# Attention heads' operands prepared one softmax earlier, and two stores moved in a queue, in a DeepNorm decoder layer

## The chip, the cores and the metric

One NeuronCore of a Trainium2 chip. The metric is the device time of one execution in microseconds, the median of three runs.

## The reference

One layer over x of 512 tokens by 1024 channels, all in float32:

- `proj = x @ w_in`, split into q, k, v (512 columns each), the pooling input (512) and two gates (1024 each).
- Branch A: causal attention, 8 heads of 64 channels, with a relative position bias. With 512 tokens and blocks of 256 the block selection keeps every earlier key, so it is plain causal softmax attention over 4 tiles of 128 queries.
- Branch B: trailing means over 2, 4, 8 and 16 tokens in four groups of 128 channels, minus the token, times a small matrix per group.
- Each branch is projected to 1024 channels (`w_branch_attn`, `w_branch_pool`), weighted by the sigmoid of its gate, and the two are added; the sum goes through `w_out`.
- `h = LayerNorm(alpha * x + ...)`; then a gated MLP of width 2816 with a causal convolution of width 3 on the gate path, and `LayerNorm(alpha * h + f)`.

## The kernel before

Every large product is made from float32 operands cut into a high and a low part (`split`: ACT copies the high part, DVE subtracts, lines 77 and 78), and is three matmuls per tile (`mm3`, lines 253, 256 and 257). Weights come in chunks of 128 x 1024 (512 KB). A chunk's raw tile is loaded by the SP queue into one of three buffers (`wraw`), split into one of five slots (`whi`, `wlo`), and used; `weights(i)` fetches up to three chunks ahead.

The order in which each engine works is settled when the kernel is built. A planner keeps a simulated clock and lets each engine take, among the instructions that it holds to be ready, the one that stands first in the program. `tc.issue_after(ins)` adds an edge to that plan: what the block issues on the engine of `ins` stands behind `ins` in that engine's queue. On the chip the engines then run their queues in this order and wait on semaphores. Queues of DMA issues (SP, ACT, POOL) are in the same plan.

**The attention stage.** For each of the 8 heads:

- `head(h)` (lines 441 to 457) makes the operands of the scores in four half-height operations: K1, the high part of k (ACT, L451), KL, the low part (DVE, L452), Q1, the high part of the scaled q (ACT, L453), with its low part in the other 64 partitions (DVE, L454). Two DMAs issued by SP (L457) copy the halves of K1 and KL into the other partitions. Q1, K1 and KL have three buffers each.
- `scores(h)` is eight matmuls, with K1 (L550) and with KL (L551), four DVE reductions that add the bias strip and take the row minimum of the negated scores (L554, the last of them is `nms[h]`), four exponentials on ACT (L559, the last is `exps[h]`), a reciprocal (L561) and four scalings on POOL (L564).
- `trans(h)` transposes the probabilities on PE (L634) and copies them out (L636 to L638); `pv(p)` multiplies a pair of heads with the values (L647, tile `ob`).
- `cover(h)` is a product of another branch put between the heads, so that PE has work during a softmax: a gate tile for the first two, then the pooling branch's projection, 12 matmuls into a bank `br` and a copy by ACT (`br_done`, L622).

The loop of line 669 runs, for h from 0 to 7: `cover(h)`, `scores(h + 2)`, `head(h + 3, nms[h + 2], exps[h + 1])`, the pair's `pv`, `trans(h)`. The last two arguments of `head` are the instructions behind which its work is put: on DVE behind the reductions of head h + 2, on ACT behind the exponentials of head h + 1.

**The last product.** The second MLP matrix is applied in seven products of 11 slices (`product`, line 1058; T3, B11, B21, T1, T2, B22, T4), each with six weight chunks. Some products load their chunks through SP into `wraw` (L236 in `fetch_fo`); others use a resident tile `tw` to which the next block of weights is added by DMAs from POOL (L241). During the sixth product the second norm's rows (scale and bias, broadcast to all partitions, tile `lnb`) are loaded by POOL (L782). Two stores issued by SP (L1107) write the bias row into rows 0 to 255 of the result, and `scale_out` later adds the normed rows to it with an accumulating DMA from POOL (L834). The last two row tiles are finished and stored without that.

Of the kernel before, what the change touches and what calls it, by code (L numbers as in the profile page):

```python
# [14 lines left out]
P = 128  # L15
# [4 lines left out]
H = 8  # L20
# [33 lines left out]
def layer_kernel(ctx: ExitStack, tc: tile.TileContext, xT, x, w_v, w_c, rel_bias, invcnt, w_group,  # L54
                 pscale, w_br, w_out, lnr, w_fi, convp, w_fo, out):
    nc = tc.nc
# [12 lines left out]
    def flip(v):  # L69
        (pst, pn), (_, n) = v.ap  # L70
        return bass.AP(tensor=v.tensor, offset=v.offset + P - 1, ap=[[pst, pn], [P, n // P], [-1, P]])

    def split(hi, lo, src, copy=None):
        if copy:
            copy(hi, src)
        else:
            state["hi"] = nc.scalar.activation(hi, src, AF.Copy)  # L77
        state["lo"] = nc.vector.tensor_tensor(lo, src, hi.bitcast(F32), op=ALU.subtract)  # L78
        return state["lo"]
# [53 lines left out]
    def slot(i, n, near=False):  # L133
        o = BESIDE if near else 0
        return tuple(wp.tile([P, SLOT], F32R, tag=f"w{q}", name=f"w{q}{i}", bufs=RING)[:, o:o + n]
                     for q in ("hi", "lo"))

    state = {"next": 0, "limit": WO0 - 1}
# [83 lines left out]
    def half(name, sl):  # L222
        return w_fo[int(name[1]) - 1, 2 - int(name[2])][:, sl]

    def piece(c):
        return slice(c * D, min((c + 1) * D, KH * S))

    def fetch_fo(i, name, c):
        sl = piece(c)
        n = sl.stop - sl.start  # L230
        step = {"T3": "=B11", "B11": "+B12", "T1": "+B22", "T2": "+B21", "T4": None}
        if name in step:
            raw = tw[:, sl]
        else:
            raw = wp.tile([P, D], F32, tag="wraw", name=f"wraw{i}", bufs=3)[:, :n]
            nc.sync.dma_start(raw, half(name, sl))  # L236
        hi, lo = slot(i, n)
        split(hi, lo, raw)
        then = step.get(name)
        if then and then[0] == "+":  # L240
            nc.gpsimd.dma_start(raw, half(then[1:], sl), accum_op=ALU.add)  # L241
        elif then:
            nc.sync.dma_start(raw, half(then[1:], sl))
        return hi, lo
# [196 lines left out]
    def head(h, *behind):  # L441
        p, e = divmod(h, 2)
        own, oth = slice(e * DH, (e + 1) * DH), slice((1 - e) * DH, (2 - e) * DH)
        qb, kb = raw_q[p], raw_k[p]
        Q1[h] = av.tile([P, S], F32R, tag="q1", name=f"q1_{h}")
        K1[h] = av.tile([P, S], F32R, tag="k1", name=f"k1_{h}")
        KL[h] = av.tile([P, S], F32R, tag="kl", name=f"kl_{h}")
        with ExitStack() as held:
            for ins in behind:
                held.enter_context(tc.issue_after(ins.ins))  # L450
            nc.scalar.activation(K1[h][own, :], kb[own, :], AF.Copy)  # L451
            nc.vector.tensor_tensor(KL[h][own, :], kb[own, :], K1[h][own, :].bitcast(F32), op=ALU.subtract)  # L452
            nc.scalar.activation(flip(Q1[h][own, :]), qb[own, :], AF.Copy, scale=DH ** -0.5)  # L453
            nc.vector.scalar_tensor_tensor(flip(Q1[h][oth, :]), qb[own, :], DH ** -0.5,  # L454
                                           flip(Q1[h][own, :]).bitcast(F32), op0=ALU.mult, op1=ALU.subtract)
        for t in (K1[h], KL[h]):
            nc.sync.dma_start(t[oth, :].bitcast(F32), t[own, :].bitcast(F32))  # L457
# [36 lines left out]
    def in_tile(kind, j):  # L494
        wh, wl = split3(weights(at[kind, j]), KT)
        b = bank(f"{kind}{j}")
        for kt in range(KT):
            mm3(b, (wh[:, kt, :], wl[:, kt, :]), (xT_hi[:, kt, :], xT_lo[:, kt, :]), kt == 0, kt == KT - 1)
        return b
# [34 lines left out]
    nms = {}  # L534
    exps = {}
# [3 lines left out]
    def scores(h):  # L539
        if h + 2 < H:  # L540
            load_strip(h + 2)
        pp = aw.tile([P, 10 * P], F32, tag="pp", name=f"pp{h}")
        nm = aw.tile([P, NT], F32, tag="nm", name=f"nm{h}")
        rs = aw.tile([P, NT], F32, tag="rs", name=f"rs{h}")
        b01 = bank(f"sc{h}_01")
        dst = [b01[:, :2 * P], b01[:, 2 * P:], bank(f"sc{h}_2")[:, :3 * P], bank(f"sc{h}_3")]
        for i in range(NT):
            n = max(2, i + 1) * P
            q = slice(i * P, (i + 1) * P)
            nc.tensor.matmul(dst[i], Q1[h][:, q], K1[h][:, :n], start=True, stop=False)  # L550
            nc.tensor.matmul(dst[i], Q1[h][:, q], KL[h][:, :n], start=False, stop=True)  # L551
        for i in range(NT):
            n = (i + 1) * P
            nms[h] = nc.vector.tensor_tensor_reduce(out=pp[:, offs[i]:offs[i] + n], in0=dst[i][:, :n],  # L554
                                                    in1=strips[h][:, S - n:], scale=1.0, scalar=3.0e38,
                                                    op0=ALU.add, op1=ALU.min, accum_out=nm[:, i:i + 1])
        for i in range(NT):
            n = (i + 1) * P
            exps[h] = nc.scalar.activation(pp[:, offs[i]:offs[i] + n], pp[:, offs[i]:offs[i] + n], AF.Exp,  # L559
                                           scale=-1.0, bias=nm[:, i:i + 1], accum_out=rs[:, i:i + 1])  # L560
        nc.vector.reciprocal(rs, rs)  # L561
        for i in range(NT):
            n = (i + 1) * P
            nc.gpsimd.tensor_scalar(pp[:, offs[i]:offs[i] + n], pp[:, offs[i]:offs[i] + n], rs[:, i:i + 1], 1.0,  # L564
                                    op0=ALU.mult, op1=ALU.mult)
        Ps[h] = pp
# [44 lines left out]
    def br_mm(f, br, b=None, ks=range(4), pin=False):  # L611
        i, o = at["br", (f, br)]
        wh, wl = (t[:, o:o + S].rearrange("p (a c) -> p a c", a=4) for t in weights(i))
        b = b or bank(f"br{f}_{br}")
        for k in ks:
            src = (zT_hi[:, k, :], zT_lo[:, k, :]) if br else (oT_hi[:, k, :], oT_lo[:, k, :])
            mm3(b, (wh[:, k, :], wl[:, k, :]), src, k == 0, k == 3, pin and k == ks[0])
        return b

    def br_done(f, br, b):  # L620
        t = branch[f, br] = unused.pop(0)
        nc.scalar.activation(t, b, AF.Copy)  # L622
# [18 lines left out]
    def pv(p):  # L641
        b = bank(f"ob{p}")
        for kb in range(NT):
            n = (NT - kb) * P
            for e in range(2):
                h = 2 * p + e
                state["pv"] = nc.tensor.matmul(b[e * DH:(e + 1) * DH, kb * P:], vv[:, kb, h * DH:(h + 1) * DH],  # L647
                                 PTs[h][:, toff[kb]:toff[kb] + n], start=kb == 0, stop=kb == NT - 1)
        split(oT_hi[:, p, :], oT_lo[:, p, :], b)
# [6 lines left out]
    def cover(h):  # L656
        with ExitStack() as held:
            if h < H - 1:
                for ins in (nms[h + 1], exps[h + 1]):
                    held.enter_context(tc.issue_after(ins.ins))  # L660
            if h < 2:
                state["limit"] = at["g", KT] + h
                nc.vector.tensor_copy(plain_gate[:, h, :], in_tile("g", h * KT))
            else:
                f = h - 2
                state["limit"] = at["br", (min(f + 3, KT - 2), 1)][0]
                br_done(f, 1, br_mm(f, 1))

    for h in range(H):
        cover(h)  # L670
        if h + 2 < H:
            scores(h + 2)
        if h + 3 < H:
            head(h + 3, nms[h + 2], exps[h + 1])
        with ExitStack() as held:
            if h and h % 2 == 0:
                pv(h // 2 - 1)
                held.enter_context(tc.issue_after(state["pv"].ins))
            trans(h)
        if h == 0:  # L680
            with tc.issue_after(nms[2].ins), tc.issue_after(exps[1].ins):
                for k in range(4):
                    split(zT_hi[:, k, :], zT_lo[:, k, :], zT[:, k, :])
# [96 lines left out]
    def ln_rows(r):  # L780
        t = hw.tile([P, 2, D], F32, tag="lnb", name=f"lnb{r}")
        nc.gpsimd.dma_start(t, bass.AP(tensor=lnr.tensor, offset=lnr.offset + r * D, ap=[[0, P], [D, 2], [1, D]]))  # L782
        nc.gpsimd.tensor_scalar(t[:, 0, :], t[:, 0, :], -0.5, None, op0=ALU.mult)
        return t

    lnb = ln_rows(0)
# [316 lines left out]
    gather(3, S, D, bank_a[1], 1, False, False)  # L1103
    product(5, bank_d, False)
    lnb = ln_rows(2)
    for i in range(2):
        nc.sync.dma_start(out[i * P:(i + 1) * P, :], lnb[:, 1, :])  # L1107
    gather_all(bank_d, (0, 0, -1, False, True))
    for i in range(2):
        scale_out(i)  # L1110
# [89 lines left out]
```

## Time and profile before

| | us |
|---|---|
| median of 3 runs | 630.85 (630.69 to 631.05) |
| the profiled execution | 631.2 |
| its span, first to last instruction | 629.5 |
| PE busy | 615.7 (98%) |
| DVE busy | 510.1 (81%) |
| ACT busy | 360.1 (57%) |
| POOL busy | 104.2 (17%) |

PE is TensorE's matmuls and PEld its weight loads; DVE, ACT, POOL and SP are the vector, scalar, GpSimd and sync engines. In rows of the timeline the columns are the start, the duration, the engine, the line, the operation, output <- inputs with shapes, and the number of instructions merged in the row; square brackets give the idle time in front of it and what ended that. A `q` behind an engine's name (SPq) is its queue of DMA issues.

### The profile page before, as it was taken

How to read it: one execution, taken by the hardware profiler on the slowest of the kernel's cores; microseconds unless marked ns; L12 is line 12 of the kernel's file. 1: busy time of each engine (PE TensorE's matmuls, PEld its weight loads, DVE VectorE, ACT ScalarE, POOL GpSimd, SP SyncE). 2: the span in 40 equal slices, each digit the busy share in tenths (PEclk: the TensorE clock that was granted, in tenths of full speed). 3: DMA queues.
4: the chain of work that ended last, by engine and by line, in shares of the span. 5: the costliest groups of instructions: out<-in, count | busy, mean ns of one | idle time of the engine just before them, and what ended most of it. 6: DMA issues, size and time to landing. Idle time of an engine off the chain costs nothing.

```text
span 629.5 us, 10658 instructions
## 1 busy us (share of the span) xinstructions
PE 615.7 (98%) x4096; PEld 555.7 (88%) x4096; DVE 510.1 (81%) x797; ACT 360.1 (57%) x554; POOL 104.2 (17%) x121
## 2 busy tenths in 40 slices
PE   9999999999999999999999999999999999999994
PEld 6899998667899998889999999999999888888874
DVE  5978778773779988399898988989887859798596
ACT  5636776764566657225575675665656347565352
POOL 0133133442010100110010101111100202123201
PEclk9999999999999999999999999999999999999998
DMA  8567643438468715805558787686834995999905
GB/s 308 170 191 190 170 124 117 135 87 306 68 201 198 185 46 192 309 25 181 121 154 192 208 197 180 192 198 176 213 85 135 313 268 126 217 211 209 260 1 134
DMA packets 43859, 110.09 MB, mean 175 GB/s; under 512 B 4496, under 2 KB 7064, under 8 KB 43552
## 3 DMA queue, kind: packets, MB, share of 16 engines
q1 hardware_dynamic: 30192, 74.65, 35.1%
q0 software_dynamic: 12896, 33.58, 27.9%
q10 hardware_dynamic: 720, 1.18, 0.5%
q8 instruction: 32, 0.52, 0.3%
q14 instruction: 19, 0.16, 0.1%
HBM read 104.13 MB, written 3.17 MB: 170 GB/s over the span
## 4 chain that ended last, share of the span: by engine, by line
PE 91%; DMA 4%; DVE 2%; issue 1%; ACT 1%; POOL 0%; SPq 0%; DVEq 0%; ACTq 0%; POOLq 0%
PE saf L253 5%; PE saf L257 5%; PE saf L256 5%; PE v L433 3%; PE fi L253 3%; PE fi L256 3%; PE fi L257 3%; PE sbf L253 2%; PE sbf L257 2%; PE sbf L256 2%; PE wo L257 2%; PE wo L256 2%; PE wo L253 2%; PE br L253 2%; PE br L256 2%; PE br L257 2%
## 5 line engine op out<-in xcount | busy, mean ns | idle before, releaser
L78 DVE TENSOR_TENSOR wlo<-araw,whi 128x1024 fp32r<-128x1024 f32 x58 | 70.4, 1224 | 5.8 <-ACT whi L77 5.3
L77 ACT ACTIVATE whi<-araw 128x1024 fp32r<-128x1024 f32 x58 | 60.6, 1056 | 20.8 <-PE saf L256 5.5
L78 DVE TENSOR_TENSOR wlo<-wraw,whi 128x1024 fp32r<-128x1024 f32 (+1 forms) x47 | 55.3, 1186 | 17.4 <-ACT whi L77 17.3
L77 ACT ACTIVATE whi<-wraw 128x1024 fp32r<-128x1024 f32 (+1 forms) x47 | 47.2, 1017 | 36.2 <-DMA wraw<-in_w_fo 13.2
L77 ACT ACTIVATE whi<-tw 128x1024 fp32r<-128x1024 f32 (+1 forms) x30 | 29.0, 981 | 21.0 <-DMA tw<-in_w_fo 9.6
L203 POOL DMA_DIRECT2D xraw<-in_w_fi x15 | 18.1, 1203 | 138.9 <-DMA xraw<-in_w_fi 105.4
L78 DVE TENSOR_TENSOR wlo<-tw,whi 128x1024 fp32r<-128x1024 f32 (+1 forms) x30 | 33.3, 1127 | 7.3 <-ACT whi L77 7.3
L253 PE MATMUL saf<-hT_hi,whi 128*128 128x256 f32 x136 | 37.9, 279 | 0.2 <-DVE saf L315 0.2
L253 PE MATMUL sbf<-T_hi,whi 128*128 128x256 f32 x136 | 38.0, 279 | 0.0
L253 PE MATMUL saf<-nT_hi,whi 128*128 128x256 f32 x136 | 37.9, 279 | 0.0
L257 PE MATMUL saf<-nT_hi,wlo 128*128 128x256 f32 x136 | 37.9, 278 | 0.0
L256 PE MATMUL saf<-hT_lo,whi 128*128 128x256 f32 x136 | 37.8, 278 | 0.0
L257 PE MATMUL sbf<-T_hi,wlo 128*128 128x256 f32 x136 | 37.8, 278 | 0.0
L256 PE MATMUL sbf<-T_lo,whi 128*128 128x256 f32 x136 | 37.8, 278 | 0.0
L256 PE MATMUL saf<-nT_lo,whi 128*128 128x256 f32 x136 | 37.8, 278 | 0.0
L257 PE MATMUL saf<-hT_hi,wlo 128*128 128x256 f32 x136 | 37.5, 278 | 0.0
L256 PE MATMUL fi<-hT_lo,whi 128*128 128x256 f32 (+1 forms) x112 | 36.3, 326 | 0.0
L257 PE MATMUL fi<-hT_hi,wlo 128*128 128x256 f32 (+1 forms) x112 | 36.3, 325 | 0.0
L253 PE MATMUL fi<-hT_hi,whi 128*128 128x256 f32 (+1 forms) x112 | 36.1, 327 | 0.0
L564 POOL TENSOR_SCALAR pp<-pp,rs 128x128 f32<-128x128 f32 (+3 forms) x32 | 23.5, 749 | 24.7 <-DVE rs L561 14.7
L77 ACT ACTIVATE whi<-xraw 128x1024 fp32r<-128x1024 f32 x15 | 15.9, 1063 | 17.7 <-PE saf L256 8.9
L253 PEld LDWEIGHTS saf<-hT_hi,whi 128*128 128x128 f32 x136 | 25.5, 188 | 0.4 <-DVE saf L315 0.4
(348 smaller groups left out, 2203.9 us busy)
## 6 DMA issues: line engine op xcount, KB each, us to landing
tw<-in_w_fo POOLq DMA_DIRECT2D x20, 512.0 KB, 9.0
araw<-in_w_fi SPq DMA_DIRECT2D x17, 512.0 KB, 4.1
xraw<-in_w_fi SPq DMA_DIRECT2D x15, 512.0 KB, 5.4
xraw<-in_w_fi POOLq DMA_DIRECT2D x15, 512.0 KB, 6.8
araw<-in_w_c SPq DMA_DIRECT2D x12, 512.0 KB, 4.0
wraw<-in_w_fi SPq DMA_DIRECT2D x10, 512.0 KB, 4.0
wraw<-in_w_fo SPq DMA_DIRECT2D x10, 512.0 KB, 8.2
tw<-in_w_fo SPq DMA_DIRECT2D x10, 512.0 KB, 7.4
```

Source lines behind the costliest of these rows:

```text
L77: state["hi"] = nc.scalar.activation(hi, src, AF.Copy)
L78: state["lo"] = nc.vector.tensor_tensor(lo, src, hi.bitcast(F32), op=ALU.subtract)
L203: state["acc"] = nc.gpsimd.dma_start(v, bass.AP(tensor=a.tensor, offset=a.offset, ap=[[pst, pn], [u.offset + S - a.offset, 2], [est, S]]), ...
L253: ins = nc.tensor.matmul(out_, wh, ah, start=start, stop=False, **kw)
L256: nc.tensor.matmul(out_, wh, al, start=False, stop=False, **kw)
L257: nc.tensor.matmul(out_, wl, ah, start=False, stop=stop, **kw)
L433: nc.tensor.matmul(bs[j], xs_[j][a], (wh, wl)[b], start=kt == 0 and n == 0, stop=False)
L564: nc.gpsimd.tensor_scalar(pp[:, offs[i]:offs[i] + n], pp[:, offs[i]:offs[i] + n], rs[:, i:i + 1], 1.0, op0=ALU.mult, op1=ALU.mult)
```

## The change

In the attention loop, `head(h + 3)` stands ahead of `scores(h + 2)` in the program, and its DVE work is put behind the reductions of head h + 1 instead of h + 2. Its ACT work stays behind the exponentials of head h + 1. In the last product, the two stores of the bias row are put behind the last `wraw` load that has been issued by then, which is the sixth chunk of the sixth product.

```diff
@@ fetch_fo
             raw = wp.tile([P, D], F32, tag="wraw", name=f"wraw{i}", bufs=3)[:, :n]
-            nc.sync.dma_start(raw, half(name, sl))
+            state["half"] = nc.sync.dma_start(raw, half(name, sl))
@@ attention loop
     for h in range(H):
         cover(h)
+        if h + 3 < H:
+            head(h + 3, nms[h + 1], exps[h + 1])
         if h + 2 < H:
             scores(h + 2)
-        if h + 3 < H:
-            head(h + 3, nms[h + 2], exps[h + 1])
         with ExitStack() as held:
@@ behind product 5
     lnb = ln_rows(2)
-    for i in range(2):
-        nc.sync.dma_start(out[i * P:(i + 1) * P, :], lnb[:, 1, :])
+    with tc.issue_after(state["half"].ins):
+        for i in range(2):
+            nc.sync.dma_start(out[i * P:(i + 1) * P, :], lnb[:, 1, :])
     gather_all(bank_d, (0, 0, -1, False, True))
```

## The prediction

> **What bounds the kernel now.** I read the page's head first, then the waits of PE, then PE's busy time in stretches, then the timeline of each engine at the two places that this leads to.
>
> ```profile
> span 629.5 us, 10658 instructions
> PE 615.7 (98%) x4096; PEld 555.7 (88%) x4096; DVE 510.1 (81%) x797; ACT 360.1 (57%) x554; POOL 104.2 (17%) x121
> PE sc L550 <- ACT zT L622: 2.9, 1, 2.9
> PE warm_ps L347 <- DVE warm L344: 1.2, 1, 1.2
> PE fod L256 <- DVE wlo L78: 0.9, 1, 0.9
> PE v L429 <- DMA wraw<-in_w_v: 0.3, 1, 0.3
> PE saf L253 <- DVE saf L315: 0.2, 1, 0.2
> ```
>
> PE is the bound: 615.7 of 629.5 us. Of the 13.8 us without it 5.5 are the five waits listed; the other 8.3 are short gaps and, for the most part, the tail behind the last matmul. Nothing that shortens another engine's work can help except in these places. Two waits lie in stages that the change touches: 2.9 us at the scores (L550) and 0.9 us in the last product (`fod`). Together they are the most that the change can take away from PE's idle time.
>
> ```profile
> 111.40:127.35 15.95, 13.08 (x77) 9.72 (x77) 11.54 (x31) 11.21 (x29) 6.31 (x9) 1.00 0.43 130
> 573.00:589.00 16.00, 16.00 (x73) 13.24 (x72) 12.46 (x13) 8.58 (x9) 6.80 (x6) 1.00 1.00 252
> ```
>
> The columns are the stretch, its length, and the busy time of PE, PEld, DVE, ACT and POOL, then the granted clock (1.00 in both), the DMA engines' busy share and GB/s. In the attention stage DVE and ACT are free for more than a quarter of the time, so the 2.87 us (15.95 - 13.08) are a matter of order, not of an engine that is full.
>
> **Part one: the operands of a head.** First, who holds PE up.
>
> ```profile
> 118.32 0.69 DVE L454 SCALAR_TENSOR_TENSOR q<-rq,q 64x512 fp32r<-64x512 f32 x1
> 119.11 0.77 PE L550 MATMUL sc<-k,q 128*128 128x256 f32 x3
> 123.56 0.28 PE L551 MATMUL sc<-kl,q 128*128 128x256 f32 x1
> 123.79 0.69 PE L551 MATMUL sc<-kl,q 128*128 128x256 f32 x3
> 124.20 0.29 DVE L554 CUSTOM_DVE_ANT_0 pp<-sc,strip 128x128 f32<-128x128 f32 x1 [2.01 <-issue]
> 125.85 0.68 DVE L452 TENSOR_TENSOR kl<-rk,k 64x512 fp32r<-64x512 f32 x1
> 126.56 0.68 DVE L454 SCALAR_TENSOR_TENSOR q<-rq,q 64x512 fp32r<-64x512 f32 x1
> 126.73 0.58 ACT L622 ACTIVATE zT<-br 128x512 f32<-128x512 f32 x1
> 127.35 0.76 PE L550 MATMUL sc<-k,q 128*128 128x256 f32 x3 [2.87 <-ACT zT L622]
> 134.31 0.69 DVE L454 SCALAR_TENSOR_TENSOR q<-rq,q 64x512 fp32r<-64x512 f32 x1
> 135.10 0.76 PE L550 MATMUL sc<-k,q 128*128 128x256 f32 x3
> ```
>
> These are heads 5, 6 and 7, the last three of eight. The bracket puts the wait down to ACT's copy of a branch bank, which ended at 127.31 us. But DVE's low part of q (L454) ended at 119.01, 127.24 and 135.00 us, and each time the scores of that head started 0.10 or 0.11 us later. So I take Q1 as the releaser; the copy only ended at about the same moment. For heads 5 and 7 PE had a branch projection to do until then; for head 6 it had nothing.
>
> How head 6 came to be late is in the same rows. Head 5's second matmuls (L551) come 4.45 us after its first. They need the low part of k, made and copied as follows.
>
> ```profile
> 112.20 0.61 ACT L453 ACTIVATE q<-rq 64x512 fp32r<-64x512 f32 x1
> 117.48 0.09 DVE L554 DVE_READ_ACCUMULATOR2_ANT nm<- 128x1 f32 x1
> 117.60 0.69 DVE L452 TENSOR_TENSOR kl<-rk,k 64x512 fp32r<-64x512 f32 x1
> 118.35 0.46 SPq L457 DMA_DIRECT2D kl<-kl  x1
> 119.84 0.61 ACT L453 ACTIVATE q<-rq 64x512 fp32r<-64x512 f32 x1
> DMA to landing us min/median/max: 2.2/2.2/4.2
> 120.72 0.48 PE L253 MATMUL br<-zT_hi,whi 128*128 128x512 f32 x1
> 121.04 0.39 PE L256 MATMUL br<-zT_lo,whi 128*128 128x512 f32 x1
> 121.27 0.40 PE L257 MATMUL br<-zT_hi,wlo 128*128 128x512 f32 x1
> ```
>
> Head 5's operands were finished on ACT at 112.81 us, but its DVE work stood behind head 4's reductions (the last read at 117.48 us), so the copy of KL left at 118.35 and landed at about 120.55 us. The plan had put the transposes and the 12 matmuls of a branch projection (120.72 to 123.56) in between. So head 5's reductions began at 124.20, and head 6's operands, queued behind them on DVE, ended at 127.24.
>
> The change adds no instruction. It moves, for five heads, two DVE operations ahead of four reductions, and with them two SP issues of 0.46 us. With head 6's DVE work behind head 4's reductions, it is ready once ACT has Q1 at 119.84 + 0.61 = 120.45 us. With the two operations (1.39 us from 125.85 to 127.24) it ends at 121.84 us, and its KL copy, 2.2 us after an issue at about 121.3, lands near 123.5. PE ran dry at 123.79 + 0.69 = 124.48. So, even if nothing else moved, all operands lie there 1.0 us before PE asks. In fact head 5's own KL lands near 116.5 (112.81 + 1.39 + 2.2), so its L551 can follow L550 directly at 119.1, and its reductions come some 2.8 us earlier, the length of the branch projection. **The wait of 2.87 us goes: -2.87.**
>
> Bounds. The most is the 2.87 plus what the split order costs: the projection's first matmul behind other work is followed after 0.32 us (120.72 to 121.04), later ones after 0.23, so 0.09 per switch; two switches fewer per head over five heads are 0.9 us. The least is zero if the bank named in the bracket is needed as well and its copy doesn't move. What is late next is that bank: with the projection last before 124.48, its copy (0.58) would end at 125.1, so 0.6 us could remain of the wait. Near the full value is likelier, as DVE's row fits three times. Of the queues that are passed: SP's copies now go ahead of loads of branch weights, 0.46 us each, hidden by the three chunks that are fetched ahead; if that cover were gone, ten issues would cost 4.6 us. The transposes are covered by the earlier softmax: head h's POOL scaling starts earlier with its reductions.
>
> DVE and ACT are not slowed by this: 4.4 us of 15.95 are free on DVE (15.95 - 11.54), and 1.4 us per head only change places.
>
> **Part two: the stores.**
>
> ```profile
> 582.13 1.22 DVE L78 TENSOR_TENSOR wlo<-wraw,whi 128x1024 fp32r<-128x1024 f32 x1
> 583.59 1.62 SPq L1107 DMA_DIRECT2D out<-lnb  x2
> 585.31 3.84 SPq L236 DMA_DIRECT2D wraw<-in_w_fo  x3
> 585.31 9.79 DMA wraw<-in_w_fo
> 595.20 1.06 ACT L77 ACTIVATE whi<-wraw 128x1024 fp32r<-128x1024 f32 x1 [7.86 <-DMA wraw<-in_w_fo]
> 596.30 1.22 DVE L78 TENSOR_TENSOR wlo<-wraw,whi 128x1024 fp32r<-128x1024 f32 x1 [5.46 <-ACT whi L77]
> 597.81 1.58 ACT L77 ACTIVATE whi<-wraw 128x1024 fp32r<-128x1024 f32 x2 [0.81 <-PE fod L257]
> 600.76 1.81 DVE L78 TENSOR_TENSOR wlo<-wraw,whi 128x1024 fp32r<-128x1024 f32 x2
> 602.02 0.50 PE L256 MATMUL fod<-wlo,sd_hi 128*128 128x512 f32 x1 [0.86 <-DVE wlo L78]
> 616.69 0.87 POOL L834 DMA_DIRECT2D out<-xs  x1 [28.49 <-ACT xs L833]
> DMA to landing us min/median/max: 3.4/8.2/11.9
> ```
>
> The last row is the landing time of the 12 loads of L236. SP's two stores waited for `lnb` until 583.59 and then held three weight loads, the first until 585.31. Its buffer was free at 583.35 (582.13 + 1.22). It landed 9.79 us later, behind 1 MB of stores, and DVE stood idle for 5.46 us, then had gathers to catch up with, so the next chunk's low part came 0.86 us late for PE. With the stores behind the three loads the first leaves at 583.4. At the median it lands at 591.6, at the fastest at 586.8, against 595.1. DVE then clears its gathers in what was idle time, and the next chunk's split is bound by its slot, which PE frees at 597.8: 597.81 + 1.06 for `whi`, 1.22 for `wlo`, is 600.1, a microsecond ahead of PE. **-0.86.** With the slowest landing, 595.3, nothing would be won; the bound on the other side is 0.86.
>
> The Trainium skill, in "DMA: Bandwidth & Descriptors", section "Issuing engines are not separate DMA queues", says that transfers interleave on the same 16 engines whichever engine issued them. The trace agrees in that the DMA engines are at 1.00 in 573 to 589 us. By that rule alone the load keeps sharing with POOL's `tw` loads and might take the 11.9 us, and the sum would be -2.87; by the median row it is -3.73.
>
> The stores themselves wait longer: behind the last load (near 588.8, the end of the three issues' row is 589.15) they leave by 590.8. The accumulating store into the same rows comes at 616.69, 26 us later, which hides them; if it did not, its wait would add to POOL's queue, with one addition for the third row tile behind it. Nothing else on SP waits: its next issue is the final store.
>
> **The sum.** The profiled execution took 631.2 us (span 629.5 and 1.7 around it): 631.2 - 2.87 - 0.86 = 627.5. The median of the runs is 0.35 lower, so 627.1. A measurement here can tell about 0.2%, 1.26 us, from no change.
>
> **The rivals.** *The plan keeps its order or the bank holds PE.* If head 5's L551 stay behind the projection, or the bank of the 126.73 copy is what L550 needs, PE waits at the same place, and only the stores' part is left: 630.85 - 0.86 = 630.0. For it speaks the bracket; against it the three intervals of 0.10 us.
>
> *The stores' part fails*, the loads landing as late as before: 630.85 - 2.87 = 628.0. For it speaks the full DMA share; against it that even 0.9 us earlier is enough.
>
> *Slower: DVE stands in front of the reductions.* DVE works in order. If KL and Q1 of head h + 3 stand ahead of head h + 2's reductions, and their ACT halves, queued behind the exponentials and weight splits, are late, the whole softmax of head h + 2 waits, five times up to 1.39 us, and the transposes behind it reach PE late. With all five exposed: 627.1 + 6.95 = 634.1. It decides from (3.73 + 1.26) / 1.39 = 3.6 heads on. Against it: ACT had Q1 at 112.81 and 120.45 us, and the reductions of the heads concerned could not start before the L550 at 119.11 or 127.35.
>
> **How the numbers follow.** Both waits gone: 0.70, at 627.1; its own range goes from 626.3 (0.8 of the 0.9 us of switches won too) to 628.2 (0.6 left at the bank, and half of the stores' part). Only the stores' part: 0.15, at 630.0. Only the operands' part: 0.05, at 628.0. Slower by the DVE queue: 0.08. Nothing at all: 0.02. From 626.3 to 630.2 the first three are taken in, some 0.81 with the likeliest one's edges off. Faster by over 0.2% is below 629.6: 0.70 + 0.05 and a little of the second, 0.77. Within it: 0.15. Slower: 0.08.
>
> **What would show it.** In the profile after: no wait of PE at L550, L551 close behind L550 for heads 4 to 7, L454 of a head several microseconds ahead of its L550, the gap near 124 us closed. At the end: SP's loads of L236 ahead of L1107, the first of them near 580.5 (583.4 less 2.9), DVE without the idle 5.46, no wait of PE for `wlo`. The prediction is wrong if L550 starts 0.04 us behind an ACT copy again, if DVE rows of L554 show idle time that ends with ACT's `k` or `q`, or if PE's busy time itself changes by more than 1 us.

## The result, and the profile after

The changed kernel took 626.62 us (median of 5 executions, 626.31 to 628.15), beside 630.85 us for the kernel before (5 executions, 629.1 to 632.97). The ratio is 0.9937, with a 95% interval of 0.9911 to 0.9963: faster by 4.2 us, where 3.7 were forecast (627.1 us). Its profiled execution took 626.3 us, with a span of 624.6.

The waits of PE, changed kernel (columns: engine, tile and line, what ended the wait, us in all, times, longest):

```profile
PE warm_ps L347 <- DVE warm L344: 1.2, 1, 1.2
PE v L429 <- DMA wraw<-in_w_v: 0.6, 1, 0.6
```

Both waits that the change was costed on are gone, the 2.9 us at the scores (L550) and the 0.9 us of `fod`.

The timeline of the changed kernel around heads 5 and 6:

```profile
115.03 0.69 DVE L454 SCALAR_TENSOR_TENSOR q<-rq,q 64x512 fp32r<-64x512 f32 x1
118.29 0.69 PE L550 MATMUL sc<-k,q 128*128 128x256 f32 x3
118.81 0.28 PE L551 MATMUL sc<-kl,q 128*128 128x256 f32 x1
119.20 0.69 DVE L454 SCALAR_TENSOR_TENSOR q<-rq,q 64x512 fp32r<-64x512 f32 x1
123.42 0.69 PE L550 MATMUL sc<-k,q 128*128 128x256 f32 x3
124.03 1.72 PE L647 MATMUL ob<-PT,vv 128*64 128x512 f32 x6
124.23 0.60 ACT L622 ACTIVATE zT<-br 128x512 f32<-128x512 f32 x1
125.68 0.38 PE L551 MATMUL sc<-kl,q 128*128 128x256 f32 x1
126.64 1.51 PE L647 MATMUL ob<-PT,vv 128*64 128x384 f32 x10
```

The low part of q (L454) is ready 2.6 us (115.72 to 118.29) and 3.5 us (119.89 to 123.42) ahead of the scores that use it, where it was 0.1 us in before. Head 5's low-part scores (L551) follow its first ones after 0.52 us instead of 4.45. Head 6's scores start at 123.42 without a wait, and ACT's copy of a branch bank, which the bracket of before had named, starts only after them (124.23). One thing is new: the eight matmuls of a pair times V (L647) are broken in two by head 6's L551.

The end, same kernel:

```profile
579.54 5.77 SPq L236 DMA_DIRECT2D wraw<-in_w_fo  x3
585.23 1.06 ACT L77 ACTIVATE whi<-wraw 128x1024 fp32r<-128x1024 f32 x1 [1.72 <-DMA wraw<-in_w_fo]
585.36 1.86 SPq L1108 DMA_DIRECT2D out<-lnb  x2
586.93 1.22 DVE L78 TENSOR_TENSOR wlo<-wraw,whi 128x1024 fp32r<-128x1024 f32 x1
591.39 1.21 DVE L78 TENSOR_TENSOR wlo<-wraw,whi 128x1024 fp32r<-128x1024 f32 x1
```

The three loads go ahead of the stores (L1108 is L1107 of before), and ACT starts on the first 5.7 us after its issue, not 9.9.

Where the time went is read from when PE comes to the same matmul in both traces. Before, then after:

```profile
100.04 0.28 PE L257 MATMUL sai<-xT_hi,wlo 128*128 128x256 f32 x1
240.04 0.28 PE L257 MATMUL sag<-gnT_hi,wlo 128*128 128x256 f32 x1
450.00 0.28 PE L257 MATMUL saf<-nT_hi,wlo 128*128 128x256 f32 x1
615.17 0.39 PE L256 MATMUL foe<-wlo,sd_hi 128*128 128x512 f32 x1
```

```profile
99.34 0.28 PE L257 MATMUL sai<-xT_hi,wlo 128*128 128x256 f32 x1
236.89 0.28 PE L257 MATMUL sag<-gnT_hi,wlo 128*128 128x256 f32 x1
446.17 0.28 PE L257 MATMUL saf<-nT_hi,wlo 128*128 128x256 f32 x1
610.17 0.39 PE L256 MATMUL foe<-wlo,sd_hi 128*128 128x512 f32 x1
```

The changed kernel is 0.70 us ahead at the first, 3.15 at the second, 3.83 at the third and 5.00 at the fourth. So 0.70 us were gained at the start, 2.45 in the attention stage, 0.68 in the MLP and 1.17 in the last product. The start and the MLP stage hold the same instructions in both. The same four rows were read in the trace of every run; the table gives the differences to the first trace of before, in us:

```
                          start   attention   MLP    last product
before, again             +0.07     +1.73    -0.29      -0.08
changed                   -0.70     -2.45    -0.68      -1.17
changed, again            -0.82     -2.44    -0.47      -1.17
changed, third            -0.89     -2.45    -0.41      -1.17
heads alone               +0.04     -2.45    -0.21      -1.17
heads alone, again        -0.37     -2.44    -0.05      -1.18
stores alone              -0.22     +1.64    -0.73      -1.17
changed, pair whole       +0.51     -3.35    -0.02      -1.17
Q1 alone                  -0.62     +0.08    -0.73      -1.17
wait filled               -0.65     +0.52    -0.68      -0.68
heads, stores by POOL     +0.14     -2.44    -0.76      -1.17
KL and stores             +1.08     -4.68    -0.01      -1.17
heads, no stores          +2.00     -2.45    -0.60      -1.17
```

### The profile page after: what moved, and what is told of

It reads as the page before. It is cut to its first block, busy times and chain, and to the rows that moved or that the text cites. A ratio compares the mean times of both kernels' runs of the same rounds, so it can differ in the third digit from the quotient of the medians.

```text
span 624.6 us, 10660 instructions
## 1 busy us (share of the span) xinstructions
PE 614.3 (98%) x4096; PEld 555.9 (89%) x4096; DVE 510.9 (82%) x797; ACT 360.6 (58%) x554; POOL 108.2 (17%) x121
## 4 chain that ended last, share of the span: by engine, by line
PE 98%; DVE 1%; DMA 1%; DVEq 0%; issue 0%
PE saf L253 5%; PE saf L256 5%; PE saf L257 5%; PE v L433 3%; PE fi L253 3%; PE fi L256 3%; PE fi L257 3%; PE sbf L253 3%; PE sbf L257 3%; PE sbf L256 3%; PE br L253 2%; PE br L256 2%; PE br L257 2%; PE wo L257 2%; PE wo L256 2%; PE wo L253 2%
## 5 line engine op out<-in xcount | busy, mean ns | idle before, releaser
L564 POOL TENSOR_SCALAR pp<-pp,rs 128x128 f32<-128x128 f32 (+3 forms) x32 | 27.0, 858 | 18.8 <-DVE rs L561 17.3
```

## The experiments

Where nothing else is said, the ratio is to the kernel before on the same chip, with its 95% interval.

**The changed kernel again, twice.** No edit.

> The changed kernel unaltered, a second time, as the yardstick for the other runs beside it. If the gain of 4.2 us (630.85 to 626.62) is all of the change, its ratio comes out at 0.993 to 0.994 again, some 626.5 us against 630.7. In the first trace pair the stages outside the change gave part of the difference: 0.7 us was already there at 6.5 us of the span, in the first projection, and 0.7 us more near 335 us in the MLP, where the trace of before shows the matmul engine out of work for 0.2 us behind a DVE addition and the trace of after doesn't. If those are variation from one run to the next, this trace's attention stage (119 to 241 us) and last product repeat to 0.1 us while the start and the MLP stage move by some tenths of a us either way. If they belong to the change, they repeat too.

> The changed kernel once more, beside the two others on the same chip, as the yardstick: 626.0 to 626.6 us, a mean clock of 0.995 or more in every execution, an attention stage 2.45 us shorter than in the first trace of before and a last product 1.17 us shorter; the start and the MLP stage as they fall.

Measured: 626.02 us (7 executions), ratio 0.9922 (0.9893 to 0.9952), and 626.60 us (6 executions), ratio 0.9922 (0.9896 to 0.9948). The attention stage and the last product repeat to 0.01 us; the start was 0.70, 0.82 and 0.89 us ahead of before's, the MLP 0.68, 0.47 and 0.41. With the other rows of the table, the start and the MLP stage are no part of the change: a second trace of before has the MLP 0.29 us earlier than the first, and kernels with the same instructions there have the start between 0.9 us earlier and 2.0 us later.

**The kernel before again.**

> The kernel before, unaltered, for a second trace of it. Two things are asked of it. First, what varies from run to run: against the first trace of before, the first projection (so far from 0.8 us earlier to 0.5 us later), the MLP stage near 335 us (0 to 0.8 us earlier), and the last product. In the last product the traces of the heads alone and of the stores alone both lie 1.17 us ahead of the first trace of before, as the changed kernel does. If the wait of 0.86 us at fod belongs to the old order of the stores, it stands here again; if it depends on when the loads happen to land, it may be gone here. Second, the clock: in the trace of the stores alone the granted clock fell to 0.58 in the 4 us behind the wait of 2.87 us, which cost 1.65 us there. If that wait is its cause, a trace of before shows either 1.00 or such a dip behind the wait, and no dip anywhere else up to the last product.

Measured: 633.39 us, in one execution. The wait of `fod` stands there again, at 0.8 us, and the attention stage is 1.73 us longer than in the first trace, with the same wait of 2.9 us in it. The clock fell behind that wait, as in the next run.

**The stores alone.**

```diff
-            nc.sync.dma_start(raw, half(name, sl))
+            state["half"] = nc.sync.dma_start(raw, half(name, sl))
...
+    with tc.issue_after(state["half"].ins):
+        for i in range(2): nc.sync.dma_start(out[i * P:(i + 1) * P, :], lnb[:, 1, :])
```

> The second part alone: the two bias stores issued behind that queue's last weight loads, the heads as before. By the prediction's term (0.86 us, the wait of fod) 630.0 us; by the distance that the last product shows between the two traces (1.15 us) 629.7 us. The wait of 2.87 us ahead of head 6's scores must be there again. Rival: the two parts are worth more together than apart (an earlier end of the attention lets the loads of the last product leave sooner too); then this run gains under 0.5 us.

Measured: 630.69 us (12 executions), ratio 0.9990 (0.9963 to 1.0017), which tells nothing from no change. The trace has the last product 1.17 us shorter and the attention stage 1.64 us longer. PE in stretches (columns: stretch, length, busy time, granted clock, DMA share, GB/s):

```profile
124.00:128.00 4.00, 1.13 (x7) 1.00 0.12 26
128.00:132.00 4.00, 4.00 (x18) 0.58 0.18 39
132.00:136.00 4.00, 4.00 (x26) 0.99 0.00 0
```

Behind the wait, which takes 2.87 of the first 4 us, the clock is at 0.58 for 4 us: 4 x 0.42 = 1.68 us of work lost, the 1.64 of the table. The first trace of before had 1.00 there. Neither theory had this. As it comes in one execution and not in the next, it blurs the times by more than the 0.86 us that was looked for.

Why one trace and not the other, the traces suggest. The changes of the clock that a trace records lie whole multiples of 3.413 us apart (in the second trace of before the fall at 128.62 us comes 36 of them behind the first record at 5.74). Cut along these steps, the first trace of before, the second, and the stores alone read:

```profile
122.34:125.75 3.41, 2.14 (x12) 1.00 0.38 144
125.75:129.16 3.41, 1.81 (x9) 1.00 0.20 43
129.16:132.57 3.41, 3.41 (x29) 1.00 0.16 34
```

```profile
125.21:128.62 3.41, 1.18 (x6) 1.00 0.18 38
128.62:132.03 3.41, 3.41 (x16) 0.50 0.18 38
```

```profile
125.23:128.64 3.41, 1.50 (x7) 1.00 0.18 38
128.64:132.05 3.41, 3.41 (x17) 0.50 0.18 38
```

In the first trace the wait falls into two steps, of which 1.27 and 1.60 us are idle (3.41 - 2.14 and 3.41 - 1.81), and the clock stays at 1.00. In the other two 2.23 and 1.91 us of one step are idle, and the next step has half the clock, which costs 3.41 / 2 = 1.71 us. So it may be where the wait falls between two steps that decides; three traces fit this, and no run was made to test it.

**The wait filled with matmuls.** The kernel before, with

```diff
+        if h == 4:
+            with tc.issue_after(state["low"].ins):      # last L551 of head 5
+                for n in range(16):
+                    nc.tensor.matmul(state["tail"], Q1[5][:, :P], K1[5][:, :2 * P], start=True, stop=True)
         if h + 2 < H:
             scores(h + 2)
```

> The kernel before with 16 more matmuls of 128x256, of head 5's operands into the unused half of a transpose bank, placed where PE waits for head 6's operands; their result is read by nobody. By the rows of L550 (0.76 us for 256 + 384 + 512 columns) they take 0.17 us each, 2.7 us in all, so they fill the wait without lengthening it. Theory: the wait itself is what makes the granted clock fall in some executions (0.58 for 4 us in the trace of the stores alone; 14 of 22 executions of before at a mean clock of 0.992 to 0.995, none of the 23 of the kernels without the wait below 0.995). Then here all executions have a clock of 0.996 or 0.997 and the median is that of the undisturbed executions of before, 629.3 to 630.2 us instead of 631.4. Rival: the clock falls for a reason outside the kernel; then the executions spread over 629 to 635 us as before's do, and the median is 631.4.

Measured: 630.37 us (12 executions, 629.22 to 631.73), ratio 0.9988 (0.9977 to 0.9999). The same stretches:

```profile
124.00:128.00 4.00, 3.03 (x22) 1.00 0.15 33
128.00:132.00 4.00, 4.00 (x33) 1.00 0.15 33
```

The mean clock of an execution, over all runs, settles whether the wait is the cause. (1.7 us lost in 629 lower it by 0.003.) It was below 0.995 in 41 of 67 executions of before and in 6 of 12 of the stores alone, which have the wait; in none of the 12 with the wait filled; and in none of 56 of the kernels that don't have it (changed, heads, KL). So the wait itself makes the clock fall, in six executions of ten. Those 41 have a median of 632.08 us, the other 26 one of 630.28: 1.8 us, near the 1.64 and 1.73 of the traces. The rival of a cause outside falls. (Q1 alone, below, has waits of about 1 us further on, and 2 of its 10 executions were below 0.995.) The 16 matmuls took 2.1 us (123.68 to 125.75) and not 2.7, and a wait of 1.0 us stayed, which did the clock no harm here. The gain is small: the stage is 0.52 us longer than in the undisturbed trace of before, and the medians beside each other differ by 0.46 us (630.37 and 630.83), above the 629.3 to 630.2 that was expected.

**The heads alone, twice.**

```diff
     for h in range(H):
         cover(h)
+        if h + 3 < H:
+            head(h + 3, nms[h + 1], exps[h + 1])
         if h + 2 < H:
             scores(h + 2)
-        if h + 3 < H:
-            head(h + 3, nms[h + 2], exps[h + 1])
```

> The first part alone: the operands of a head held behind the reductions of one softmax sooner; the two bias stores stay where they were. By the prediction's term (2.87 us, the whole wait ahead of head 6's scores) 628.0 us. By the traces of before and after, which lie 2.45 us apart over the attention stage, 628.4 us: 2.87 won, 0.78 given back where the 64-column matmuls of a pair are broken up, and some tenths won back elsewhere. The wait of 0.9 us of the last product (fod behind wlo) must be there again in its trace. If the start and MLP differences of the first trace pair belong to the first part, the time is 627.0 to 627.7 us instead.

> The heads' part alone, unaltered, a second time. What is still open is what the stores' part is worth when the heads' part is there. By times, the heads alone had a median of 627.75 us (10 executions) against 626.57 of the changed kernel (18 executions), 1.18 us apart; by its one trace the last product was as short as in the changed kernel (1.17 us ahead of before), with no wait at fod, and 0.8 us of margin between the last split and PE. Theory one: the margin is small, and in other executions the load lands later and the wait is back; then this trace or the spread shows it: a wait at fod of 0.3 to 0.9 us here, or a median of 627.4 to 628 again with the trace an early one. Theory two: the stores' part is worth nothing beside the heads' part, and the 1.18 us were the start, which lay between 0.9 us earlier and 2.0 us later than before's in the traces; then the last product is 1.17 us ahead again, without a wait, and the median may be anything from 626 to 628.

Measured: 627.75 us (10 executions), ratio 0.9939 (0.9917 to 0.9961), and 627.47 us (6 executions), ratio 0.9938 (0.9916 to 0.9960). The attention stage is 2.45 us shorter, as in the changed kernel. But the last product is 1.17 us shorter too, with the stores where they were. The end of the first of these traces:

```profile
580.90 0.95 SPq L1107 DMA_DIRECT2D out<-lnb  x2
581.94 4.58 SPq L236 DMA_DIRECT2D wraw<-in_w_fo  x3
590.96 1.06 ACT L77 ACTIVATE whi<-wraw 128x1024 fp32r<-128x1024 f32 x1 [6.24 <-DMA wraw<-in_w_fo]
```

The load still comes behind the stores and reaches ACT after 9.0 us. On PE's scale (2.62 us ahead of before at this place) that is 593.58 where before had 595.20: 1.6 us sooner, and 0.86 was all that PE lacked. The second trace shows the same, without a wait. So in these two traces the stores' part would have had nothing to win.

That isn't the doing of the heads' part. Q1 alone, below, leaves the stores where they were, has an attention stage as long as before's, and has no wait at `fod` either. The second trace of before and the wait filled have

```profile
PE fod L256 <- DVE wlo L78: 0.8, 1, 0.8
PE fod L256 <- DVE wlo L78: 0.2, 1, 0.2
```

From 182 us on, the six traces with the stores ahead of the loads (before twice, heads alone twice, Q1 alone, wait filled) have the same instructions in the same order on every engine, and waits of 0.9, 0.8, 0, 0, 0 and 0.2 us. The load reached ACT 9.9, 10.1, 9.0, 9.2, 8.5 and 9.0 us after its issue. So the wait comes and goes with the landing of the load, and why it landed earlier in four of them isn't shown. In the eight traces with the stores behind the loads, issued by POOL or left out, there is no wait.

The times of heads alone and of the changed kernel differ: 627.7 us over these 16 executions, 626.6 over 18 of the changed kernel. In the traces that difference lies ahead of the stores, at the start and in the MLP stage, where both programs are alike. Whether it is that chance, or the wait at `fod` coming back in executions that were not traced, stays open.

**Q1 alone.** The kernel before, with

```diff
         with ExitStack() as held:
             for ins in behind: ...            # K1 and KL, as before
+        with ExitStack() as held:
+            for ins in q_behind: ...          # Q1's two: nms[h + 1] in place of nms[h + 2]
```

> The kernel before with only the two Q1 operations of a head held behind one softmax sooner; K1, KL and so the low-part scores stay as late as before, and the copy of the branch bank (ACT, L622) keeps its place. It asks which of the two released head 6's scores in before: DVE's low part of q, which ended 0.11 us ahead of them, or ACT's copy of the bank, which ended 0.04 us ahead. If Q1 alone: no wait at head 6's first scores, PE goes on at about 124.5 us (on the scale of the first trace), and the time falls by some 2 to 2.9 us, unless KL, still late, makes a wait of its own further on. If the bank holds as well: the scores start where the copy ends, at about 127.3 us again, with a wait of 2.8 us, and the time stays within 0.3 us of before.

Measured: 631.06 us (10 executions), ratio 1.0000 (0.9980 to 1.0020). A wait of PE, then rows of its timeline (L553, L554, L625 and L637 are L550, L551, L622 and L634 of before):

```profile
PE tr L637 <- POOL pp L567: 1.1, 1, 1.1
```

```profile
123.02 0.69 PE L554 MATMUL sc<-kl,q 128*128 128x256 f32 x3
123.55 0.69 PE L553 MATMUL sc<-k,q 128*128 128x256 f32 x3
125.97 0.57 ACT L625 ACTIVATE zT<-br 128x512 f32<-128x512 f32 x1
130.38 0.28 PE L554 MATMUL sc<-kl,q 128*128 128x256 f32 x1
138.16 0.36 PE L554 MATMUL sc<-kl,q 128*128 128x256 f32 x1
```

Two answers. Head 6's scores start without a wait at 123.55, 3.0 us before the copy of the bank ends (126.54): Q1 was the releaser, and the bank held nothing up. And the stage is not shorter (+0.08 us). The low-part scores stay 7.8 us apart (130.38 to 138.16), since each head's KL is made behind the reductions of the head before, and these need that head's low-part scores. Part of the wait moved to the end of this loop, where the last transposes wait 1.06 us for the last softmax, and 0.4 us to a weight split behind the loop. Most of the rest is PE's busy time, 1.09 us more in the stage than in before (138.22 against 137.13), as the matmuls come in another order; that I haven't taken apart.

**KL and the stores.** The counterpart: `head(h + 3)` stands behind `scores(h + 2)` as in before, with `k_behind` (nms[h + 1]) for K1 and KL and Q1's two behind nms[h + 2], and the stores are moved.

> The kernel before with the stores' part of the change, and of the heads' part only the K1 and KL operations held behind one softmax sooner; Q1's two stay where they were in before. The counterpart of the run with Q1 alone, which lost the wait at head 6's scores and still gained nothing in the attention stage (0.06 us longer), as the low-part scores went on 7.7 us apart and the last softmax came as late as before. Theory: the low part of k is what the order hangs on. With KL early the low-part scores follow the first ones directly, the reductions come early, and Q1, queued behind them on DVE, is early too: no wait at L553 of head 6, the attention stage shorter by 2.45 us as in the changed kernel, and by another 0.8 to 0.9 us since the second pair's eight matmuls stay whole in this order. Time 625.6 us beside 626.3 for the changed kernel. Rival: Q1, released by DVE 0.11 us ahead of the scores in before, still ends behind the reductions; then a wait of 1 to 2.9 us stands at L553 again and the time is 627.5 to 629.5 us.

Measured: 625.19 us (6 executions, 624.22 to 626.19), ratio 0.9897 (0.9871 to 0.9923), against 0.9922 for the changed kernel beside it. No wait of PE in the stage, which is 4.68 us shorter: the 2.87 of the wait, and 1.81 us less of PE's busy time than in before (135.32 against 137.13). The rival falls; so does the size, as 3.3 were expected. By its median this is the best version here.

**The pair whole.** The changed kernel, with head 6's low-part scores behind the second pair's product (the edit in short; `mm(i, K1, ...)` is the matmul of row tile i with K1):

```diff
+            for i in (0, 2, 3): mm(i, K1, False)
+            between()                         # pv(1), for head 6
+            with tc.issue_after(state["pv"].ins):
+                mm(0, KL, True); mm(1, K1, False); mm(1, KL, True); mm(2, KL, True); mm(3, KL, True)
```

> The changed kernel with one thing altered: the low-part scores of head 6 issued behind the eight 64-column matmuls of the second pair's P times V instead of between its third and fourth. In the trace of after those eight take 1.65 + 1.44 = 3.09 us in two pieces, in before 2.31 us in one. If a broken pair costs that, this gives 0.78 us, so 625.8 us beside 626.6, and the eight take 2.3 us. Rival one: the second piece was long for another reason (operand or bank), and they take 3 us whole as well; no gain. Rival two: the reductions of head 6, behind 0.66 us later low-part scores, make the next softmax late, and the gain is given back at the transposes or at head 7's scores as a wait of PE of 0.3 to 0.8 us.

Measured: 626.08 us (6 executions), ratio 0.9918 (0.9886 to 0.9949), not to be told from the changed kernel by its time. The trace tells: its stage is 0.90 us shorter than the changed kernel's. The rows of L647, first the second and the last pair in before, then the second pair with the pair whole, then both pairs in the run of KL and stores (L659 and L650 there; the trace counts each matmul twice):

```profile
128.04 2.37 PE L647 MATMUL ob<-PT,vv 128*64 128x512 f32 x16
152.57 1.07 PE L647 MATMUL ob<-PT,vv 128*64 128x512 f32 x2
155.40 2.37 PE L647 MATMUL ob<-PT,vv 128*64 128x512 f32 x14
```

```profile
125.25 2.37 PE L659 MATMUL ob<-PT,vv 128*64 128x512 f32 x16
```

```profile
126.60 2.38 PE L650 MATMUL ob<-PT,vv 128*64 128x512 f32 x16
150.21 2.38 PE L650 MATMUL ob<-PT,vv 128*64 128x512 f32 x16
```

Start to next start, eight matmuls take 2.31 us when they are whole (128.04 to 130.35 in before, 125.25 to 127.55 in this run). Broken after the third, with five other matmuls in between, they take 1.65 + 1.44 = 3.09 in the changed kernel. Before's last pair was broken after the first, with seven in between, and took 1.01 (152.57 to 153.58) + 2.30 (155.40 to 157.70) = 3.31. The two heads of a pair write the two halves of the output's partitions. In a whole product the two heads' matmuls of a block of keys start 0.01 us apart (128.04 and 128.05 in before); in a broken one the matmul ahead of the break runs alone, and those behind it beside one of another length or alone. The Trainium skill has the concurrency, in "TensorE: Matmul & The Clock Gate", Part 3 (small matmuls on disjoint tiles of the array run at the same time); that other matmuls put between partners undo part of it, for the rest of the pair too, is what these rows add. Of the 2.23 us by which KL and stores beats the changed kernel in this stage, 0.78 is the second pair and 1.00 the last one; the other 0.45 I haven't taken apart.

**The stores by POOL, and no stores.** Both with the heads' part: `nc.gpsimd.dma_start(out[...], lnb[:, 1, :])` for the two stores, or neither of them.

> The first part alone, with the two bias stores issued by POOL instead of SP, at the same point of the program. It asks what made the last weight loads land late in before (9.8 us after their issue, against 5.6 us in after): that SP was held by the stores, or that 1 MB of stores shared the DMA engines with them. If holding SP is it, the first of the three loads leaves at 579.5 us on the scale of after and lands 5.5 to 6 us later, DVE has no idle stretch of 4 to 5 us ahead of its split, and the time is that of the changed kernel, 626.0 to 626.6 us. If the bytes are it, the load leaves as early but lands 8 to 10 us later, and the time is that of the heads alone, 627.7. Either way, POOL's own loads stand behind stores that wait for the scaled bias rows; if that delays them past the split of the following chunk, a wait of PE at fod or fo_cut shows it and the time is above 628.

> The heads' part alone, and the two bias stores left out altogether (rows 0 to 255 of the result lack the bias part). It asks how much of the last product's loss is the stores. In the four traces where the stores stood ahead, the first of SP's last three loads reached ACT 8.9 to 10.1 us after its issue; behind the loads, 5.7 to 6.2 us; by POOL's queue 5.2 us. If the stores' 1 MB ahead of it was the cause, the load lands here within 6 us and the time is at or a little under that of the changed kernel, 626.0 to 626.6 us; if POOL's loads share the engines with it just as much, it lands after 8 us or more and the time is that of the heads alone, 627.7 us.

Measured: 627.15 us (4 executions), ratio 0.9928 (0.9910 to 0.9947), and 627.55 us (6 executions), ratio 0.9928 (0.9899 to 0.9956). The load reached ACT 5.2 and 5.6 us after its issue. In the six traces with the stores behind the loads that took 5.7 to 6.2 us, and once 7.5; in the six with the stores ahead 8.5 to 10.1. So the stores ahead are what made it late. The run with POOL doesn't tell holding SP from sharing the engines: POOL issued the stores at 581.75 us, after SP's load (581.15). The times don't follow the landing: 626.0 to 626.6 us was expected for an early one, and both lie within the spread of the heads alone (626.5 to 629.8 us). No wait at `fod` was there to win in the traces of the heads alone, and the trace without stores lost 2.00 us at the start.

## Why the prediction came out

**Q1 as the releaser of head 6's scores: right,** and shown. The run with Q1 alone has no wait there, with the bank's copy ending 3.0 us later. "What is late next is that bank", 0.6 us, did not come.

**-2.87 for the wait: right mechanism, mis-sized by 0.42.** The wait went whole, but PE's busy time in the stage rose by 0.42 us (137.13 to 137.55), so the stage gained 2.45. Given back were 0.78 where head 6's L551 broke up the second pair, which the prediction had no term for; the other 0.36 (2.45 - 2.87 + 0.78) may be the fewer switches of order of its bound, which no run takes apart. What the prediction told as a side effect, that head 5's KL lands early and its L551 follow directly, was the cause that counted: Q1 alone lost the wait and gave all of it back further on, and KL, with Q1's own place in the queue left as it was, gained all of it and more.

**-0.86 for the stores: the wait went, but it isn't always there to win.** The load left at 579.54 us, when its buffer came free (578.30 + 1.22), landed after 5.6 us, within the range of 3.4 to 11.9, and DVE worked on through the place where it had stood idle for 5.46 us. The last product gained 1.17, all of it at this wait: 0.86 idle, and 0.31 that the matmuls around it took longer in before, which the term had left out. By the rule of the Trainium skill in "DMA: Bandwidth & Descriptors", "Issuing engines are not separate DMA queues", the load was to share the engines with POOL's and might have taken 11.9 us, and nothing would have been won; the engines were full (busy share 1.00 from 579.54 to 585.13 us), and it took 5.6. The step that failed is to take the wait of one trace as a fixed price of the old order: of the six traces that keep this order, both of before have it, one has 0.2 us of it and three have none, the heads alone among them. The rival "the stores' part fails" gave 628.0 us, near the 627.7 of the heads alone, but by another mechanism: there the load was still late (9.0 and 9.2 us after its issue, 9.9 in before), and PE didn't wait.

**The granted clock, taken as 1.00: the term left out.** It costs before 1.64 to 1.73 us in six executions of ten, some 1.05 us on average (41/67 x 1.7). With it the parts come near the whole: 2.45 + 1.17 + 1.05 = 4.67, and the medians over the runs, 631.36 (67 executions of before) and 626.57 (18 of the changed kernel), are 4.79 apart. It is a rough balance, as the start and the MLP stage, which gave 1.38 us between the first two traces, are left out, and the 1.17 stands in both traces of before but needn't in each of its executions. The forecast of 3.73 fits the executions whose clock stayed up: 630.28 - 626.57 = 3.71. That it fits so well is partly luck, with one term 0.42 too large and the other 0.31 too small.

**The rivals.** The plan keeping its order fell with the contiguous L551. DVE ahead of the reductions: head 7's KL did wait 0.47 us for ACT's k, ahead of head 6's reductions, and no wait of PE came of it. "PE's busy time itself changes by more than 1 us" was named as a sign of error, and it fell by 1.4 us (615.7 to 614.3). By stage it is 0.99 us less at the start, 0.46 in the MLP and 0.31 in the last product, and 0.42 more in the attention stage. Most of it lies where both programs are alike and varies from run to run: a sign badly chosen.

## What to carry to other kernels

Look for the operand that closes the loop from one head to the next (here KL, through the reductions and the low-part scores), and not only for the one that ended last before a wait: freeing the last alone moved the wait down the loop. Price a wait of PE with the clock behind it; filling it kept the clock up here, for a gain of some 0.5 us. Take a wait that hangs on when a load lands from several traces, not from one. Keep matmuls that run side by side next to each other in the order: five and seven other matmuls between partners cost 0.8 and 1.0 us here.

## What the hardware showed that was not expected

- A wait of 2.87 us made the granted clock fall to 0.50 for 3.41 us (0.58 over 4 us) in some executions and not in others of the same kernel (41 of 67 by the mean clock); with 2.1 us of it filled and 1.0 us left, in none of 12. The Trainium skill, in "TensorE: Matmul & The Clock Gate", "What's actually happening", has a free-running window of about 3.4 us that halves the clock once it was idle. Length and size fit: 3.41 us at 0.50. That a gap shorter than the window is enough is what the runs add; in three traces 1.91 and 2.23 us of idle time in one step of 3.41 us were enough, and 1.60 us was not.
- The start of the kernel, up to the first projection's weights, lay between 0.89 us ahead of and 2.00 us behind the first trace of before, with the same instructions. Differences of a microsecond between single executions of this kernel mean nothing until the trace shows where they lie.
